# Masked softmax on one core: GpSimd in place of SyncE as the engine that opens and closes the first critical section

## The chip, the cores and the metric

The kernel runs on one core of a Trainium2 chip. The metric is the device time of one launch in microseconds (us). The core has five engines with an instruction stream each: PE (TensorE), DVE (VectorE), ACT (ScalarE), POOL (GpSimd) and SP (SyncE, which computes nothing and here issues transfers). [...] Transfers between the device memory and the on-chip memory are issued from SP, ACT or POOL and are carried out by 16 DMA engines that all of these share.

## The reference

```python
batch, heads, seq_q, seq_k = 16, 8, 256, 256
x       = randn(batch, heads, seq_q, seq_k)           # float32
lengths = randint(seq_k // 2, seq_k, size=batch)      # int32
result  = zeros_like(x)
for b in range(batch):
    n = lengths[b]
    m = x[b, :, :, :n]
    e = exp(m - max(m, axis=-1))
    result[b, :, :, :n] = e / sum(e, axis=-1)
```

Each row of 256 values is a softmax over its first `lengths[b]` values, and zero behind them. The input and the output have 33.55 MB each.

## The kernel before

**Tiling.** One batch is 2048 rows of 256 float32 values, 2 MB. It lies in the on-chip memory as 128 partitions with 16 rows each (`nt = 16`). The tile `xt` has eight slots, each for one batch, so that loads run ahead of the arithmetic and stores behind it. Everything is done in place in `xt`.

**Arithmetic.** For a batch DVE clips the columns from 128 on with a ramp (`down`, line 231, plus the length, line 248), so that what lies behind the length becomes a huge negative number. ACT takes the exponential (lines 374 and 377), for twelve of the sixteen rows of a partition with the row's sum beside it; DVE sums the other four (line 269). DVE then takes the reciprocal (line 279) and multiplies (line 282). In the first batch it clips and waits by halves.

**Transfers.** The lengths come in by one small transfer on ACT's queue (line 142). The first batch comes in as two halves on SP's queue (line 145). The next three come on POOL's queue (line 196), behind a memset (line 191) that waits until DVE has the lengths as a tile (`len_s`, line 239; on the way there lie a cast on DVE, line 236, and a small matmul, line 216). All later loads are issued by POOL in a loop (lines 205 to 211) which reads the length of the batch and branches to one of twelve transfers that differ in the number of columns loaded (line 168). A load waits until the store that last used its slot is done. All 39 stores are issued by SP (line 154), each behind a wait for DVE's multiplication.

**The order around the change.** The order of instructions on each engine is that of the program text, and all waits are written out by hand. For this the kernel's body stands in a critical section (line 106), in which the framework adds no waits of its own. At its two ends, however, the framework adds a few instructions, and they carry line 106 in the profile:

- Opening: one engine, here SP, executes a NOP that increments a semaphore of this engine. Every engine, SP too, then has a branch into the section, and the branch waits for that semaphore (these branches carry line 433).
- Closing: when the opening engine has done its own part of the body, it increments a second semaphore. Every engine has, behind its own part, a drain that waits for this second semaphore and then increments a semaphore of its own; for POOL it is a NOP in place of the drain, because of `no_gpsimd_drain=True`. The opening engine waits for all of these, and executes a closing NOP.

Ahead of the section stands a barrier over all engines (line 422): the four others report to POOL, and POOL then releases them. Behind the section stands a second one, opened and closed by SP, that holds a single wait:

```python
    with tc.tile_critical(no_gpsimd_drain=True):
        nc.sync.wait_ge(s_last, 64)
```

`s_last` counts the stores of the last batch. After it comes the closing barrier of the program (line 433), again with POOL as the engine to which the others report.

The body of the section starts like this on the three engines that issue transfers:

```python
        nc.scalar.dma_start(out=word64, in_=lengths[None, :]).then_inc(s_word, 16)
        for h in range(2):
            s = slice(h * half, (h + 1) * half)
            nc.sync.dma_start(out=xt[:, 0, s], in_=x_f[batch_of(0), :, s]).then_inc(s_ld[h], 16)
...
        nc.gpsimd.iota(
```

SP's part of the body ends with waits for the stores of all batches but the last (lines 157 to 159). POOL's part ends with its last load. ACT and DVE end with a test of the sums that, for this input, leaves a branch untaken (lines 333 and 384).

Of the kernel before, what the change touches and what calls it, by code (L numbers as in the profile page):

```python
# [17 lines left out]
POOL = mybir.EngineType.Pool  # L18
# [3 lines left out]
def kernel(  # L22
# [80 lines left out]
    s_late = sem("s_late")  # L103
    s_last = sem("s_last")
    n_st = [64 * (len(range(par, late, 2)) + 2) for par in range(2)]
    with tc.tile_critical(no_gpsimd_drain=True):  # L106
        s_word = sem("s_word")
        s_ones = sem("s_ones")
        s_lenb = sem("s_lenb")
# [328 lines left out]
```

## Time and profile before

| what | value |
|---|---|
| time, median of 3 runs | 154.49 us (154.41 to 154.68) |
| span of the profiled execution, first to last instruction | 152.8 us |
| the profiled execution's own time | not given; its span lies 1.7 us under the median |
| bytes moved by DMA | 61.57 MB, 403 GB/s over the span |
| DVE, ACT, POOL busy | 134.6, 95.1, 21.3 us |

The profile is that of one execution. An engine's name with a small q behind it (SPq, POOLq) means its sequencer: semaphore instructions, branches, NOPs, drains and the issuing of transfers, which are not counted as busy time. In the view by stretches the DMA share is the time that the packets begun in a stretch took, over that of 16 engines; a full stretch shows about 1.0 and can be a little over it. In the source view a row gives the engine, the instruction, its count, its shortest, median and longest duration in ns, and the starts of the first and the last one in us; a view that is cut to a stretch has only the instructions that run in it.

### The profile page before, as it was taken

The numbers are of one execution on the slowest core, as the hardware profiler recorded it, in microseconds if no ns is written. First come the engines' busy times: TensorE is split into PE (matmuls) and PEld (weight loads), VectorE is DVE, ScalarE is ACT, GpSimd is POOL, SyncE is SP. The second block draws the span as 40 slices with busy tenths as digits, with TensorE's granted clock in tenths as the row PEclk, the third lists the DMA queues.
The fourth block names the chain that finished last, engine by engine and source line by source line (L and its number), as shares of the span: only waits on it lengthen the run. The fifth ranks groups of instructions, "written<-read, shape, count | busy, mean of one in ns | idle before, by whom it ended". The sixth has DMA issues, their size and how long they took to land.

```text
span 152.8 us, 818 instructions
## 1 busy us (share of the span) xinstructions
PE 0.3 (0%) x2; PEld 0.2 (0%) x2; DVE 134.6 (88%) x107; ACT 95.1 (62%) x402; POOL 21.3 (14%) x29
## 2 busy tenths in 40 slices
PE   0000000000000000000000000000000000000000
PEld 0000000000000000000000000000000000000000
DVE  1369999999999999999999999999999999999500
ACT  3096699339394967859393939577593939395000
POOL 4962110030303020030300220302000000000000
DMA  4999999999999999999999999999999999999994
GB/s 107 420 446 433 401 435 347 421 445 420 394 397 422 405 421 411 411 409 405 419 411 418 408 399 419 408 410 423 417 421 419 413 420 422 435 435 442 429 410 187
DMA packets 10646, 61.57 MB, mean 403 GB/s; under 512 B 898, under 2 KB 1010, under 8 KB 7058
## 3 DMA queue, kind: packets, MB, share of 16 engines
q1 hardware_dynamic: 5904, 35.65, 56.7%
q0 software_dynamic: 4736, 25.89, 41.9%
q14 instruction: 4, 0.03, 0.1%
q10 hardware_dynamic: 2, 0.00, 0.0%
HBM read 27.98 MB, written 33.55 MB: 403 GB/s over the span
## 4 chain that ended last, share of the span: by engine, by line
DVE 87%; DMA 5%; issue 1%; SPq 0%; PE 0%
DVE xt L282 48%; DVE xt L248 23%; DVE row_sum L269 12%; DMA xt<-in_x_dram 5%; DVE inv_sum L279 3%; DVE ends L317 0%; SPq L145 0%; DVE bad L320 0%; PE count L218 0%; DVE redo L328 0%; SPq L433 0%; SPq L106 0%
## 5 line engine op out<-in xcount | busy, mean ns | idle before, releaser
L377 ACT ACTIVATE xt<-xt 128x256 f32<-128x256 f32 x192 | 76.6, 400 | 0.2 <-DVE xt L248 0.2
L282 DVE TENSOR_TENSOR xt<-xt,inv_sum 128x2048 f32<-128x2048 f32 x32 | 73.3, 2292 | 1.1
L374 ACT ACTIVATE xt<-xt 128x1024 f32<-128x1024 f32 x16 | 16.9, 1056 | 42.8 <-DVE xt L248 42.8
L248 DVE SCALAR_TENSOR_TENSOR xt<-down,len_s,xt 128x2048 f32<-128x2048 f32 (+1 forms) x17 | 37.7, 2219 | 5.0 <-DMA xt<-in_x_dram 5.0
L377 ACT ACTIVATION_READ_ACCUMULATOR xt<-xt 128x1 f32 x192 | 35.9, 187 | 0.0
L168 POOL DMA_DIRECT2D xt<-in_x_dram x12 | 13.2, 1104 | 84.0 <-DMA xt<-in_x_dram 62.3
L269 DVE TENSOR_REDUCE row_sum<-xt 128x4 f32<-128x1024 f32 x16 | 19.4, 1210 | 0.0
L279 DVE RECIPROCAL inv_sum<-row_sum 128x8 f32<-128x8 f32 x32 | 6.3, 198 | 0.5
L191 POOL MEMSET xt<- 128x1536 f32 x4 | 5.4, 1398 | 1.1 <-DVE len_s L239 1.1
L361 ACT ACT_TABLE_LOAD x1 | 1.3, 1283 | 1.6 <-SPq L106 1.6
L196 POOL DMA_DIRECT2D xt<-in_x_dram x3 | 1.8, 590 | 0.0
L231 DVE TENSOR_SCALAR down<-iota_i 128x256 f32<-128x256 int32 x1 | 0.3, 300 | 1.6 <-POOL iota_i L181 1.6
L317 DVE TENSOR_REDUCE ends<-inv_sum 128x1 f32<-128x256 f32 x2 | 0.7, 408 | 0.0
L236 DVE CAST len_b<-word 1x16 bf16<-1x16 int32 x1 | 0.2, 164 | 0.4 <-DMA word<-in_lengths_dram 0.4
L239 DVE TENSOR_SCALAR len_s<-len_f 128x16 f32<-128x16 f32 x1 | 0.2, 176 | 0.3 <-PE len_f L216 0.3
L218 PE MATMUL count<-bad,ones_c 128*1 128x3 bf16 x1 | 0.2, 165 | 140.8 <-DVE bad L320 140.8
L181 POOL IOTA iota_i<- 128x256 int32 x1 | 0.3, 331 | 0.6 <-SPq L106 0.6
L328 DVE TENSOR_REDUCE redo<-count 1x1 f32<-1x3 f32 x1 | 0.1, 150 | 0.3 <-PE count L218 0.3
L320 DVE TENSOR_SCALAR bad<-ends 128x1 bf16<-128x1 f32 x3 | 0.3, 150 | 0.0
L187 POOL MEMSET seed<- 1x1 f32 x2 | 0.2, 225 | 0.0
L218 PEld LDWEIGHTS count<-bad,ones_c 128*1 128x1 bf16 x1 | 0.1, 79 | 140.8 <-DVE bad L320 140.8
L361 ACT ACTIVATE warm<-const-float32-0.0 128x1 f32<-128x1 f32 x1 | 0.2, 204 | 0.0
(10 smaller groups left out, 1.1 us busy)
## 6 DMA issues: line engine op xcount, KB each, us to landing
out_dram<-xt SPq DMA_DIRECT2D x20, 1024.0 KB
xt<-in_x_dram POOLq DMA_DIRECT2D x4, 2048.0 KB, 16.3
out_dram<-xt SPq DMA_DIRECT2D x15, 512.0 KB
xt<-in_x_dram POOLq DMA_DIRECT2D x3, 1728.0 KB, 16.7
out_dram<-xt SPq DMA_DIRECT2D x2, 2048.0 KB
xt<-in_x_dram POOLq DMA_DIRECT2D x2, 1600.0 KB, 16.0
xt<-in_x_dram POOLq DMA_DIRECT2D x2, 1280.0 KB, 14.7
xt<-in_x_dram SPq DMA_DIRECT2D x2, 1024.0 KB, 6.4
```

Of the source, the lines that this page charges most:

```text
L168: nc.gpsimd.dma_start(out=xt[:, slot, :, :w], in_=x_n[:, b, :, :w]).then_inc(s_sw[par], 16)
L191: nc.gpsimd.memset(xt[:, b, :, low:], 0.0).then_inc(s_fill, 1)
L196: nc.gpsimd.dma_start(out=xt[:, b], in_=x_f[batch_of(b)]).then_inc(s_sw[b - 1] if b < 3 else s_ld[2], 16)
L218: nc.tensor.matmul(count, lhsT=ones_c, rhs=bad, start=True, stop=True).then_inc(s_count, 1)
L248: return nc.vector.scalar_tensor_tensor(out=t, in0=down[:, None, lo:hi].to_broadcast([P, s.stop - s.start, hi - lo]), scalar=len_s[:, batc ...
L269: nc.vector.tensor_reduce(out=row_sum[:, b % slots, :lump], in_=xt[:, b % slots, :lump, :], op=ALU.add, axis=AX,).then_inc(s_exp[0], 1)
L279: step(nc.vector.reciprocal(out=inv_sum[:, b, s], in_=row_sum[:, b % slots, s]))
L282: nc.vector.tensor_tensor(out=t, in0=t, in1=inv_sum[:, b, s, None].to_broadcast([P, half, seq_k]), op=ALU.mult,).then_inc(s_out, 1)
L317: step(nc.vector.tensor_reduce(out=ends[:, k : k + 1], in_=values, op=op, axis=AX))
L361: nc.scalar.activation(out=warm, in_=nc.const_aps.tensor(0.0, (P, 1), F32), func=EXP)
L374: nc.scalar.activation(out=e, in_=e, func=EXP).then_inc(s_lump, 1)
L377: ins = nc.scalar.activation(out=e, in_=e, func=EXP, accum_out=row_sum[:, slot, j : j + 1])
```

## The change

The first section is told to use POOL for its opening and closing; the second section, and everything inside the first, is the same.

```diff
-    with tc.tile_critical(no_gpsimd_drain=True):
+    with tc.tile_critical(sync_engine=POOL, no_gpsimd_drain=True):
         s_word = sem("s_word")
         s_ones = sem("s_ones")
         s_lenb = sem("s_lenb")
```

So the opening NOP, the increment with which the closing starts, and the closing NOP with its waits go from SP's instruction stream to POOL's, and the branches into the section wait for a semaphore of POOL. Each engine keeps its drain (POOL its NOP) at the end of its part.

## Prediction

> **What bounds the kernel now.** I read the page first, then the stretches by time, then the waits of DVE and of SP's queue, and last the chain of waits at the two ends of the run, because the change touches only the ends. The page gives the span, the engines and the bytes.
>
> ```profile
> span 152.8 us, 818 instructions
> PE 0.3 (0%) x2; PEld 0.2 (0%) x2; DVE 134.6 (88%) x107; ACT 95.1 (62%) x402; POOL 21.3 (14%) x29
> DMA packets 10646, 61.57 MB, mean 403 GB/s; under 512 B 898, under 2 KB 1010, under 8 KB 7058
> ```
>
> ```profile
> DVE 87%; DMA 5%; issue 1%; SPq 0%; PE 0%
> ```
>
> ```profile
> 143.74 0.15 DVE redo L328
> ```
>
> DVE is the busiest engine, and the chain of waits puts 87% of the span on it. The last piece of that chain (second fence: start, duration, what) ends at 143.9 us, though, nine microseconds before the span does. The stretches show what fills them (columns: stretch and its length, busy time and count for PE, PEld, DVE, ACT and POOL, clock, DMA share, GB/s).
>
> ```profile
> 2.00:2.10 0.10, 0.00 (x0) 0.00 (x0) 0.00 (x0) 0.10 (x1) 0.00 (x0) 1.00 0.00 0
> 2.10:2.20 0.10, 0.00 (x0) 0.00 (x0) 0.00 (x0) 0.10 (x1) 0.00 (x0) 1.00 1.36 246
> 2.00:4.00 2.00, 0.17 (x1) 0.10 (x1) 0.34 (x2) 1.13 (x2) 0.95 (x1) 1.00 0.93 246
> 4.00:6.00 2.00, 0.00 (x0) 0.00 (x0) 0.00 (x0) 0.00 (x0) 2.00 (x4) 1.00 0.98 410
> 6.00:8.00 2.00, 0.00 (x0) 0.00 (x0) 1.28 (x1) 0.22 (x1) 2.00 (x3) 1.00 1.07 455
> 20.00:24.00 4.00, 0.00 (x0) 0.00 (x0) 3.96 (x4) 4.00 (x16) 0.03 (x1) 1.00 0.92 370
> 30.00:90.00 60.00, 0.00 (x0) 0.00 (x0) 59.28 (x44) 40.91 (x175) 8.09 (x7) 1.00 1.02 413
> 90.00:140.00 50.00, 0.00 (x0) 0.00 (x0) 49.38 (x37) 35.08 (x150) 3.45 (x3) 1.00 1.02 420
> 146.00:150.00 4.00, 0.00 (x0) 0.00 (x0) 0.00 (x0) 0.00 (x0) 0.00 (x0) 1.00 1.00 422
> 150.00:151.00 1.00, 0.00 (x0) 0.00 (x0) 0.00 (x0) 0.00 (x0) 0.00 (x0) 1.00 0.72 303
> ```
>
> The reader is to see the next-to-last number: the 16 DMA engines start moving x between 2.1 and 2.2 us and are then full, at a share of about 1.0, until past 150 us, while all compute engines stand still after 146. So the **bytes** set the end: when they start, and at what rate they go. DVE is nearly as full, and it also begins with those bytes:
>
> ```profile
> DVE xt L248 <- DMA xt<-in_x_dram: 5.0, 2, 3.5
> SPq L433 <- DMA out_dram<-xt: 4.2, 1, 4.2
> ```
>
> DVE's only waits for x are the two halves of the first batch. SP's last wait, 4.2 us, is for the last stores. Whichever of the two one takes as the bound, it hangs on the instant at which SP issues the first x load, and that instant is where the change works. The chain of waits between 0.5 and 1.2 us has it (start, duration, what):
>
> ```profile
> 0.85 0.05 issue
> 0.90 0.01 SPq L106
> 0.92 0.06 issue
> 0.98 0.03 SPq L433
> 1.01 0.12 issue
> 1.14 0.39 SPq L145
> ```
>
> SP is let out of the program's first barrier at about 0.84 (its barrier instruction takes 17 ns by its row below and ends at 0.85), executes the NOP of line 106 at 0.90, passes its own branch into the section at 0.98 and issues the first load at 1.14. The first data follow 0.96 to 1.06 us after that.
>
> **The entry, part by part.** The barrier is opened by GpSimd itself. In the source view of line 422, cut to 0.80 to 0.81 us, the second of GpSimd's barrier instructions is what runs, and cut to 0.80 to 0.85 us it has SP's; the view of line 433 cut to 0.94 to 0.95 us has GpSimd's branch, and cut to 0.93 to 0.95 us ACT's; line 106, over the whole span, has a NOP of each of the two engines.
>
> ```profile
> L422 POOLq EVENT_SEMAPHORE  x1: 17/17/17, 0.8 to 0.8; - x1
> L422 SPq EVENT_SEMAPHORE  x1: 17/17/17, 0.8 to 0.8; - x1
> L433 POOLq COMPARE_BRANCH  x1: 38/38/38, 0.9 to 0.9; - x1
> L433 ACTq COMPARE_BRANCH  x1: 38/38/38, 0.9 to 0.9; - x1
> L106 SPq NOP  x2: 13/13/13, 0.9 to 147.3; - x2
> L106 POOLq NOP  x1: 17/17/17, 147.0 to 147.0; - x1
> ```
>
> So GpSimd frees the others at about 0.80, SP hears of it 0.04 later, and then the opening signal goes back the same way: SP's NOP at 0.90, the branches of ACT and GpSimd at 0.94. The change takes out that second crossing for SP. GpSimd's NOP comes one sequencer step after its barrier instruction; SP's step there is 0.05 (the "issue" row), and I take 0.05 to 0.07, which puts the NOP at 0.86 to 0.88. With 0.04 of crossing the signal is at SP at 0.90 to 0.92. SP, without a NOP of its own, is ready for its branch at 0.85 + 0.05 = 0.90. Its branch then stands at 0.90 to 0.92 in place of 0.98: **0.06 to 0.08 earlier, I take 0.07**. The 4 ns by which GpSimd's NOP is longer is inside that rounding. Both ends: no more than 0.08 can be gained, because SP is not ready before 0.90; and nothing is lost, because GpSimd stood at its branch by 0.94 at the latest, so its NOP cannot be later than that and the signal is at SP by 0.98, as now. The two load issues, the 39 stores behind them on SP's queue and DVE's first mask all move with SP.
>
> The other engines: ACT's branch goes from 0.94 to 0.90 to 0.92, so the load of the lengths, issued on ACT, is about 0.03 earlier. GpSimd now waits for its own signal; SP's own took 0.08 from NOP to branch, so GpSimd's branch is at 0.87 + 0.08 = 0.95, 0.01 later, and up to 0.08 later at the bound above. Behind it on GpSimd are the iota, three kinds of small memset and the first large memset. The lines that wait on them:
>
> ```profile
> POOL xt L191 <- DVE len_s L239: 1.1, 1, 1.1
> DVE down L231 <- POOL iota_i L181: 1.6, 1, 1.6
> DVE len_b L236 <- DMA word<-in_lengths_dram: 0.4, 1, 0.4
> ```
>
> GpSimd waits 1.1 us for the lengths before its first large memset, and DVE, after the mask ramp that needs the iota, waits 0.4 us for the lengths. Those waits hide 0.01 to 0.08; if the cover were gone the price would be those same hundredths. The loads that GpSimd issues behind that memset depend on the lengths, which come 0.03 sooner.
>
> **The exit.** GpSimd now gives the closing signal when its own part is done, after its last load, and its NOP collects the drains of the others; SP keeps its drain. The section can still not be closed before SP has left it, since GpSimd's NOP waits for SP's drain. Rows of the source views of lines 106, 205 and 433, the last cut to 147.3 to 152.2 us:
>
> ```profile
> L205 POOLq COMPARE_BRANCH  x6: 34/48/50, 19.6 to 106.4; - x6
> L106 SPq DRAIN  x1: 7/7/7, 147.1 to 147.1; - x1
> L106 SPq EVENT_SEMAPHORE  x3: 17/28/28, 147.0 to 147.2; - x3
> L433 SPq EVENT_SEMAPHORE  x3: 28/28/4155, 147.4 to 147.6; - x3
> L433 POOLq DRAIN  x1: 478/478/478, 147.1 to 147.1; - x1
> ```
>
> GpSimd leaves its loop at 106.4 and has nothing else to do. All of the closing lies between 147.0 and 147.4, and behind it SP waits from 147.6 for 4.155 us for the last store. One signal may cross once more or once less, 0.04, and several waits move from SP's queue to GpSimd's, where only the drain of 0.478 us stands behind them, ending near 147.6. All of it is inside the 4.155 us, so I cost it at nothing. Without that cover the whole closing is worth 0.4 us. The second section is still opened and closed by SP, so what follows the last store, from 151.7 on, stays as it is.
>
> **Sum.** Entry 0.07 earlier, exit 0. The profiled span of 152.84 us becomes 152.77. The profiled execution's own time is not shown, so I take the 1.65 us between its span and the median of 154.49 as unchanged: 154.49 - 0.07 = **154.42 us**. The runs shown reach from 154.41 to 154.68, so 0.07 is not to be told from no change; about 0.2%, 0.31 us, is what a measurement of this kernel can tell.
>
> **Rivals.** First, no gain: GpSimd reaches its NOP only by 0.94, or the compiler's placement leaves SP's branch where it was; then 154.49. For it speaks that no row shows GpSimd's idle sequencer between 0.82 and 0.94.
>
> Second, slower: the lengths fall behind x. Today ACT's issue goes ahead of SP's:
>
> ```profile
> 1.09 0.52 ACTq L142 DMA_DIRECT2D word<-in_lengths_dram  x1
> 1.14 0.86 SPq L145 DMA_DIRECT2D xt<-in_x_dram  x2
> 4.37 1.76 POOL L196 DMA_DIRECT2D xt<-in_x_dram  x3
> ```
>
> The lead is 0.05 now and about 0.01 afterwards (1.06 against 1.07). If SP gets ahead and the two can't issue at once, the lengths are late by SP's first issue, 0.39 us, and with them GpSimd's memset and its three loads, at 4.37 now. SP's two loads are 2 MB together; the stretches move 0.49 + 0.82 + 0.91 = 2.22 MB by 8 us, so GpSimd's data are already flowing just before 8 us. If they come 0.39 later, the DMA engines run dry for that long: 154.49 + 0.39 = 154.88. [...] Against it: the two issues overlap today, and the lead, though small, stays on ACT's side.
>
> [...]
>
> Third, more gained than the start: the stretch from 20 to 24 us, where the first stores meet the end of the opening loads, runs at share 0.92 and 370 GB/s in place of 1.02 and 413. At 413 it would be 4 x (1 - 370/413) = 0.42 us shorter: 154.42 - 0.42 = 154.00. Against it: loads and stores both move by 0.07, so their relative order has little reason to change.
>
> **How the numbers follow.** Forecast 0.58, no gain 0.12, lengths late 0.14, the stretch mended 0.16. Of the forecast's share, 0.04 is given to runs that scatter past the 0.31 us on the fast side. That makes faster 0.20, within 0.2% 0.66, slower 0.14. The range reaches to both outer cases, 154.0 to 154.9; the likeliest one's own is 154.41 to 154.49 by the bounds 0.08 and 0, and with the scatter of the runs shown 154.3 to 154.65.
>
> **What would show it.** Right: GpSimd's NOP near 0.87, SP's branch near 0.91 and its first load near 1.07, first data 0.07 earlier, DMA share about 1.0 up to 150 us, SP's last wait still above 4 us. The lengths' rival shows as DVE's wait for them growing from 0.4 towards 0.8 and a gap in the DMA share near 8 us. The third shows as a share of 1.0 between 20 and 24 us. The forecast is wrong if SP's first load does not move, if the last wait of SP shrinks towards nothing, or if the rate in the long stretches shifts by more than the 0.2% that would drown the 0.07.

## The result, and the profile after

The changed kernel is **slower** by a little: 154.79 us against 154.63 us (medians of 13 runs each, in turn on one chip), a ratio of 1.0017 with a 95% interval of 1.0009 to 1.0025. Over all runs whose span is on record, on several chips, the median is 154.77 us (36 runs) against 154.53 us (128 runs of the kernel before).

The entry did what the prediction worked out. The chain of waits of the changed kernel between 0.5 and 1.2 us (start, duration, what):

```profile
0.74 0.06 issue
0.80 0.02 POOLq L422
0.82 0.06 issue
0.88 0.03 POOLq L106
0.91 0.02 issue
0.92 0.03 SPq L433
0.95 0.12 issue
1.08 0.39 SPq L145
```

GpSimd's NOP stands at 0.88, SP's branch at 0.92 where it was at 0.98, and the first x load at 1.08 where it was at 1.14. The stretches of the changed kernel show that the data follow: between 2.10 and 2.20 us there is more than twice the traffic of before (573 against 246 GB/s), and the long stretches run at the same rates.

```profile
2.10:2.20 0.10, 0.00 (x0) 0.00 (x0) 0.00 (x0) 0.10 (x1) 0.00 (x0) 1.00 3.34 573
20.00:24.00 4.00, 0.00 (x0) 0.00 (x0) 3.97 (x3) 3.97 (x18) 0.54 (x1) 1.00 0.96 380
30.00:90.00 60.00, 0.00 (x0) 0.00 (x0) 59.27 (x44) 40.91 (x175) 8.08 (x7) 1.00 1.02 413
146.00:150.00 4.00, 0.00 (x0) 0.00 (x0) 0.00 (x0) 0.00 (x0) 0.00 (x0) 1.00 1.00 424
```

The closing is with GpSimd now. Line 106 of the changed kernel:

```profile
L106 POOLq NOP  x3: 13/17/17, 0.9 to 147.2; - x3
L106 POOLq EVENT_SEMAPHORE  x3: 17/43/43, 107.1 to 147.1; - x3
L106 PEldq DRAIN  x1: 218/218/218, 143.0 to 143.0; - x1
L106 ACTq DRAIN  x1: 8/8/8, 144.3 to 144.3; - x1
L106 DVEq DRAIN  x1: 17/17/17, 144.5 to 144.5; - x1
L106 SPq DRAIN  x1: 7/7/7, 147.0 to 147.0; - x1
```

GpSimd gives the closing signal at 107.1 us, the drains follow at 143.0 to 147.0 where in the kernel before they all stand at 147.0 to 147.1, and the closing NOP stands at 147.2 where SP's stood at 147.3.

The end differs in two ways. First, the source view of line 433, SP alone, from 151.9 us on: the kernel before,

```profile
L433 SPq DRAIN  x3: 7/7/7, 152.1 to 152.4; - x3
L433 SPq EVENT_SEMAPHORE  x2: 17/17/17, 152.3 to 152.8; - x2
```

and the changed kernel:

```profile
L433 SPq EVENT_SEMAPHORE  x3: 17/17/28, 152.1 to 152.9; - x3
L433 SPq DRAIN  x3: 7/7/7, 152.2 to 152.5; - x3
```

SP has one semaphore instruction more behind the last store. It names semaphores that SP has waited for already at 147.3 us, and it starts 0.04 us behind the end of the instruction ahead of it. The same instruction is in the trace of a kernel below in which ACT opens and closes the first section, and in none in which SP does. So it comes with the collecting of the drains on another engine; why the framework adds it is not shown.

Second, the time that isn't in the span at all. Each run has its time and its span; time minus span is what a launch takes outside the instructions that the profile lists:

| | runs | median time | median span | time minus span, mean (standard deviation) |
|---|---|---|---|---|
| kernel before | 128 | 154.53 | 152.8 | 1.68 (0.06) |
| changed kernel | 36 | 154.77 | 152.9 | 1.87 (0.03) |

The spans are nearly level (means 0.07 us apart), which fits 0.06 us gained at the entry and about 0.07 lost behind the last store. The gain is not to be seen at the end of this pair of executions: SP's branch behind the last store stands at 151.7 us in both. The loss of 0.19 us lies **outside** the instructions that the profile shows. One row of the trace hints at it: the transfer view of the kernel before, cut to 154.4 to 154.5 us, 1.6 us behind its last profiled instruction, has one transfer of the kind that the profile names `instruction`, called a fetch from here on (82 GB/s over the 0.1 us, so 8 KB),

```profile
q14 instruction: 1, 0.01, 33.2%
```

and the changed kernel, cut to 151.4 to 156 us, has no transfer at all behind its end.

```profile
DMA packets 0, 0.00 MB, mean 0 GB/s; under 512 B 0, under 2 KB 0, under 8 KB 0
```

### The profile page after: what moved, and what is told of

It reads as the page before. It is cut to its first block, busy times and chain, and to the rows that moved or that the text cites. A ratio compares the mean times of both kernels' runs of the same rounds, so it can differ in the third digit from the quotient of the medians.

```text
span 152.9 us, 819 instructions
## 1 busy us (share of the span) xinstructions
PE 0.3 (0%) x2; PEld 0.2 (0%) x2; DVE 134.7 (88%) x107; ACT 95.0 (62%) x402; POOL 21.3 (14%) x29
## 4 chain that ended last, share of the span: by engine, by line
DVE 87%; DMA 5%; issue 1%; SPq 0%; PE 0%; POOLq 0%
DVE xt L282 48%; DVE xt L248 23%; DVE row_sum L269 12%; DMA xt<-in_x_dram 5%; DVE inv_sum L279 3%; DVE ends L317 0%; SPq L145 0%; DVE bad L320 0%; PE count L218 0%; DVE redo L328 0%; SPq L433 0%; POOLq L106 0%; POOLq L422 0%
```

## Experiments

All comparisons are with runs of the kernel before on the same chip, in turn. "Length" is the number of SP's instructions in the compiled program: 79 before, 75 in the changed kernel, because the opening NOP, the closing increment and the collecting of the drains went to GpSimd and one wait came in at the end. The traces list two fewer each, 77 and 73. Added instructions are increments of semaphores that nobody waits for; they are called hidden where SP would wait anyway.

### First four: control, repeat, and two ends

The control is the kernel before, unedited.

> The kernel before, once more, as a control. Every theory: the ratio to the kernel before is 1.000 with its interval around it. The profile adds a second sample of what the trace of before showed: first x load on SP at 1.14 us, first data between 2.1 and 2.2 us, DVE's last piece near 143.7, SP's wait for the last store over at 151.7 us, span 152.8 us. What differs between this profile and the first is what one execution scatters by.

Ratio 0.9992 (0.9979 to 1.0005), median 154.56 us against 154.56; its profiled execution has a span of 153.1, so 0.3 us is what one execution scatters by.

The changed kernel, unedited.

> The changed kernel once more, on the chip of the other three. Tail theory (the one further semaphore instruction of SP behind the last store, 0.06 us, is all that the change costs, and the earlier entry isn't carried to the end): ratio 1.0004, SP's wait for the last store over at 151.7 us. Early-load theory (loading x 0.06 us earlier brings DVE's chain and the stores forward, and the mixed traffic then runs slower): ratio 1.001 to 1.002, last store at 151.7 us or later although the data start 0.07 us earlier.

Ratio 1.0019 (1.0001 to 1.0036), median 154.72 against 154.56, time minus span 1.88. The loss repeats.

```diff
+        nc.sync.sem_inc(s_pad[0], 1)
         for h in range(2):
             s = slice(h * half, (h + 1) * half)
```

> The changed kernel with one semaphore instruction of SP, about 0.06 us, ahead of its two x loads, so that these are issued at 1.14 us as in the kernel before; the longer tail stays. Tail theory: no faster than the changed kernel, 1.0004 against the kernel before. Early-load theory: the 0.1 to 0.2 us come back and 0.06 us of tail are left, 1.0004 as well, but 0.001 less than the changed kernel run beside it.

The first load went to 1.18 us; ratio 1.0015 (0.9993 to 1.0038), median 154.80, time minus span 1.85. Nothing came back, and the time outside the span, where no load runs, is as long as in the changed kernel. So nothing speaks for the theory that early loads slow the traffic; the interval is too wide to exclude the 0.001 that it asked for.

```diff
         nc.sync.wait_ge(s_last, 64)
+        for k in range(4):
+            nc.sync.sem_inc(s_pad[k], 1)
```

> The kernel before with four more semaphore instructions of SP behind its wait for the last store, and nothing else. Tail theory: each costs one step of the sequencer, 0.06 to 0.07 us, whole: the span is 0.24 to 0.28 us longer, ratio 1.0016 to 1.0018. If what stands behind the last store is hidden by something (the other engines' part of the closing barrier): ratio 1.000.

Ratio 1.0036 (1.0025 to 1.0048): 0.55 us, twice the expectation. The source views of lines 408 and 436 (the closing barrier in this file), SP alone, say why:

```profile
L408 SPq EVENT_SEMAPHORE  x4: 17/17/17, 151.7 to 151.9; - x4
L436 SPq EVENT_SEMAPHORE  x5: 17/17/28, 152.0 to 153.5; - x5
L436 SPq DRAIN  x3: 7/7/130, 152.6 to 153.2; - x3
```

The steps take 0.07 us each (three from 151.7 to 151.9; the first increment rides on the wait for the last store). Three waits that in the kernel before stand ahead of that wait came behind it here (five semaphore instructions of line 436 in place of the two shown above), so there are six steps more and not four, about 0.4 us. And one drain, 130 ns in place of 7, came late. That stall was expected by no theory. Time minus span was 1.63, the smallest so far. Both together led to the next question: does the length of a stream decide?

### Second four: whose length

```diff
                 pick(v_len, bass.ds(b, 1), bass.ds(n % slots, 1), par, widths + [seq_k], landed)
+        for k in range(4):
+            nc.gpsimd.sem_inc(s_pad[k], 1)
```

> The kernel before with four more semaphore instructions of GpSimd behind its last load, where it is idle from 106 us on; with the branch that they bring its stream is five instructions longer, as in the changed kernel. The runs so far put the loss of 0.16 us outside the profiled span: time minus span is on average 1.67 to 1.73 us for the kernel before and 1.87 to 1.88 for the changed one. Theory that the length of GpSimd's stream makes it: time minus span 1.87, ratio 1.001. Theory that the length of SP's stream makes it: 1.70, ratio 1.000.

Ratio 0.9998 (0.9984 to 1.0012), time minus span 1.67. GpSimd's length does not bring the loss.

```diff
+        for k in range(4):
+            nc.sync.sem_inc(s_pad[k], 1)
         for par in range(2):
             nc.sync.wait_ge(s_st[par], n_st[par])
```

> The changed kernel with four more semaphore instructions of SP ahead of its waits for the stores (line 157), where it waits for 3.9 us; its stream is then as long as in the kernel before. Length of SP's stream: time minus span falls from 1.87 to 1.70 and the time to that of the kernel before. Length of GpSimd's stream, or neither: time minus span stays at 1.87, ratio 1.001.

Ratio 0.9999 (0.9985 to 1.0012), 154.52 against 154.51 us, time minus span 1.71. **Four idle instructions on SP remove the whole loss**; the changed opening and closing are still there.

```diff
-    with tc.tile_critical(no_gpsimd_drain=True):
+    with tc.tile_critical(sync_engine=ACT, no_gpsimd_drain=True):
```

> ACT opens and closes the first section in place of SP. SP's stream is as short as in the changed kernel, GpSimd's as in the kernel before, ACT's five instructions longer. Length of SP's stream: time minus span 1.87. Length of GpSimd's: 1.70. Tail theory: the span has the same further semaphore instruction behind the last store as the changed kernel, 0.06 us.

Ratio 1.0031 (1.0005 to 1.0056), median 154.82, time minus span 1.87. The same loss outside, with GpSimd's stream as long as before. (The ratio is pulled up by four long runs of twelve; the profiled one is one of them, with a span of 154.3.)

The four hidden instructions of the last but one kernel, in the kernel before:

> The kernel before with four more semaphore instructions of SP ahead of line 157, hidden there. The run with four instructions behind the last store had a time minus span of 1.63 and, in its profile, a stall of SP of about 0.3 us inside the closing barrier. Length of SP's stream: the same again, time minus span 1.63, and the stall in the closing barrier, with nothing added behind the last store; ratio 1.001 to 1.002. Otherwise: ratio 1.000 and no stall.

Ratio 1.0026 (1.0011 to 1.0040), time minus span 1.62, and the stall is there. Line 436 on SP, cut to 152.3 to 152.8 us, and the kernel before at the same place (line 433, cut to 152.3 to 152.5):

```profile
L436 SPq EVENT_SEMAPHORE  x1: 17/17/17, 152.3 to 152.3; - x1
L436 SPq DRAIN  x1: 130/130/130, 152.7 to 152.7; - x1
```

```profile
L433 SPq EVENT_SEMAPHORE  x1: 17/17/17, 152.3 to 152.3; - x1
L433 SPq DRAIN  x1: 7/7/7, 152.4 to 152.4; - x1
```

The drain behind the same semaphore instruction starts 0.3 us later, and takes 130 ns. Nothing but the number of SP's instructions ahead of it was changed.

### Third four: does the stall move as counted?

Hidden instructions ahead of line 157 again, now 17 in the kernel before and 21 and 12 in the changed one:

> The kernel before with 17 semaphore instructions of SP hidden ahead of line 157, which makes its stream 96 instructions long in place of 79. Theory of the boundary: at one fixed place of SP's instruction stream SP stalls for about 0.3 us; with 83 instructions it lay in front of SP's last drain of the closing barrier, so each instruction added ahead moves it one instruction earlier, and with 96 it lies before the wait for the last store, where SP waits 4 us anyway. Then time minus span is 1.62, the span has no stall, and the time is 0.05 to 0.1 us below the kernel before, ratio 0.9995. Rival (the effect comes and goes with the length in some other way): time minus span 1.7 or more, or a stall in the closing barrier.

> The changed kernel with 21 hidden semaphore instructions of SP, 96 as well. Boundary theory: time minus span 1.62 in place of 1.87, no stall in the span, ratio 0.9995 to 1.000 against the kernel before and 0.15 to 0.25 us below the changed kernel. Compared with the other run of 96 instructions it shows the change without the boundary: entry 0.06 us earlier and tail 0.06 us longer, together nothing; 0.06 us slower if the entry isn't carried to the end. Rival: 1.70 or 1.87 outside.

> The changed kernel with 12 hidden semaphore instructions of SP, 87 in all. Boundary theory: the boundary lies between the wait for the last store and the closing barrier, so the profile shows a gap of about 0.3 us on SP there, four instructions earlier than with 83, time minus span 1.62, ratio 1.001 to 1.002: slower than with 79 and than with 96. Rival (longer is better): between the times of 79 and 96.

The place was right in all three traces. With 87 (12 hidden in the changed kernel), lines 409 and 436 on SP, the second cut to 152.7 to 153.2 us:

```profile
L409 SPq NOP  x1: 17/17/17, 152.6 to 152.6; - x1
L436 SPq EVENT_SEMAPHORE  x1: 28/28/28, 153.0 to 153.0; - x1
L436 SPq DRAIN  x2: 7/22/37, 153.1 to 153.2; - x2
```

A gap of 0.4 us in front of the sixth instruction from the end, as counted. With 96 in the kernel before, line 107 on SP from 146 to 148.5 us has its three semaphore instructions, which span 147.0 to 147.2 in the kernel before, stretched over 0.6 us:

```profile
L107 SPq EVENT_SEMAPHORE  x3: 17/28/28, 146.9 to 147.6; - x3
```

Time minus span was 1.62 in all three, as expected. The times were not: 154.99 us and 1.0035 (1.0022 to 1.0049) for the first, 155.07 and 1.0035 (1.0023 to 1.0047) for the second, where 0.9995 to 1.000 was expected; 154.99 and 1.0029 (1.0019 to 1.0040) for the third, where 1.001 to 1.002 was. With 96 the stall is hidden behind SP's 4 us wait and outside nothing is lost, but the span is 0.6 us longer (means 153.40 and 153.43 against 152.78).

The fourth tested whether the start of the loads reaches the end. Its four instructions stand ahead of the x loads, 13 more ahead of line 157:

> The kernel before with four semaphore instructions of SP ahead of its first x load and 13 hidden ones, 96 in all: the first x load is issued 0.27 to 0.4 us later. If the start of the loads is carried whole to the end: the span is 0.27 to 0.4 us longer than in the other run of the kernel before with 96. If the end does not follow the start: the span is the same.

The loads on SP's timeline, the kernel before with 96 first:

```profile
1.14 0.86 SPq L146 DMA_DIRECT2D xt<-in_x_dram  x2
```

```profile
1.42 0.86 SPq L148 DMA_DIRECT2D xt<-in_x_dram  x2
```

0.28 us later; the mean span is 153.72 against 153.40 with the same length (five runs each), 0.32 longer. The start is **carried whole** to the end.

### Fourth four: the stall far from the end

Hidden instructions behind the two x loads, where SP is idle for 12 us, 40 in the kernel before and 44 in the changed one:

```diff
             nc.sync.dma_start(out=xt[:, 0, s], in_=x_f[batch_of(0), :, s]).then_inc(s_ld[h], 16)
+        for k in range(40):
+            nc.sync.sem_inc(s_pad[k % 8], 1)
```

> The kernel before with 40 semaphore instructions of SP behind its two x loads, where it is idle from 2 to 14 us; its stream has 119 instructions. Boundary theory: the stall and the instruction fetch that follows it lie among SP's stores in the middle of the run, where SP waits for DVE and one 8 KB fetch is nothing. Then time minus span 1.62, no gap on SP behind the last store, no fetch behind 120 us, and the time 0.05 to 0.1 us below the kernel before, ratio 0.9993 to 0.9997. If the stall is not tied to a place in the stream: 1.000 or more.

> The changed kernel with 44 such instructions at the same place, 119 as well. Boundary theory: time minus span 1.62, and the change's loss is gone: the same as the other run with 119 to within 0.06 us, 0.2 to 0.3 us below the changed kernel. If the loss lies in what the change itself does (the opening, the closing, the order of the first loads): still 0.15 us above the other run with 119.

And 27 ahead of line 157 in the kernel before, 106 in all:

> The kernel before with 27 hidden instructions ahead of line 157, 106 in all, where 17 made it slower by 0.5 us although the stall was hidden. Theory of the late fetch (there the 8 KB fetch ran at 150.9 us, among the last stores, and one of the 16 DMA engines reported the last store about 0.45 us after the others): the stall moves among the hidden instructions near 144 us, the fetch to about 147 us, the straggler goes, and the time is 0.05 to 0.1 us below the kernel before. Rival (the hidden instructions themselves, or a long stream, delay the end): slower by 0.5 us as with 17.

The changed kernel stood beside them once more:

> The changed kernel again, on the chip of these three, for the comparison. All theories: ratio 1.001 to 1.002, time minus span 1.87, no instruction fetch behind 120 us in the trace.

The last came out as expected: 1.0019 (1.0000 to 1.0038), 1.86 outside. The other three had their stall where it was counted, at 94.2, 85.6 and 144.3 us, and their fetch 3.4 us or less behind its end: the kernel before with 119 has a fetch at 97.8 us and none behind 120. Outside, they lost nothing (1.61, 1.64, 1.61). In time all three missed: 155.20 us and 1.0041 (1.0027 to 1.0055), 155.11 and 1.0035 (1.0023 to 1.0046), 154.92 and 1.0016 (0.9995 to 1.0036). With equal lengths the changed kernel does not show the loss of 0.16 to 0.27 us: it is 0.09 us below the kernel before with 119 (155.11 against 155.20) and 0.08 above with 96 (155.07 against 154.99). With five to seven runs each, 0.1 us is not resolved; that the time outside is level (1.64 against 1.61, 1.62 in both with 96) says more.

What else is new in them can be seen in the transfer views from 10 to 152 us, the kernel before and then the one with 119, and in the stretches of the latter at its end:

```profile
q14 instruction: 4, 0.03, 0.1%
```

```profile
q14 instruction: 5, 0.04, 0.1%
```

```profile
151.00:151.20 0.20, 0.00 (x0) 0.00 (x0) 0.00 (x0) 0.00 (x0) 0.00 (x0) 1.00 0.00 0
151.20:151.40 0.20, 0.00 (x0) 0.00 (x0) 0.00 (x0) 0.00 (x0) 0.00 (x0) 1.00 0.11 41
151.40:151.60 0.20, 0.00 (x0) 0.00 (x0) 0.00 (x0) 0.00 (x0) 0.00 (x0) 1.00 0.00 0
151.60:151.80 0.20, 0.00 (x0) 0.00 (x0) 0.00 (x0) 0.00 (x0) 0.00 (x0) 1.00 0.10 41
```

41 GB/s over 0.2 us is one packet of 8 KB. Single packets still start behind 151.2 and 151.6, after nearly all the traffic is over; the kernel before starts none of this size after 151.0:

```profile
151.00:151.20 0.20, 0.00 (x0) 0.00 (x0) 0.00 (x0) 0.00 (x0) 0.00 (x0) 1.00 0.01 0
151.20:151.40 0.20, 0.00 (x0) 0.00 (x0) 0.00 (x0) 0.00 (x0) 0.00 (x0) 1.00 0.01 0
```

All six kernels with a fifth fetch ahead of the end of the last store have median spans 0.4 to 0.7 us longer than the kernel before beside them (for the one with late x loads, without their 0.3). It is not shown that the fetch does it. Late single packets do not go with it: the kernel before with 96 has the fetch and none of them (first line), and the changed kernel with 87 has them (the other two) although its fetch comes only at 153.6 us, behind the last store.

```profile
151.20:151.40 0.20, 0.00 (x0) 0.00 (x0) 0.00 (x0) 0.00 (x0) 0.00 (x0) 1.00 0.01 0
```

```profile
151.20:151.40 0.20, 0.00 (x0) 0.00 (x0) 0.00 (x0) 0.00 (x0) 0.00 (x0) 1.00 0.10 41
151.40:151.60 0.20, 0.00 (x0) 0.00 (x0) 0.00 (x0) 0.00 (x0) 0.00 (x0) 1.00 0.10 41
```

The median span with 87 is 0.6 us longer as well, of which the stall is about 0.4. A rival, that many added instructions lengthen the run by themselves, was not separated from the fetch. What lengthens these spans stays open.

### Last two: between 75 and 83

Seven and six hidden instructions ahead of line 157 in the changed kernel:

> The changed kernel with 7 hidden semaphore instructions of SP ahead of line 157, 82 in all. By the count (83: the stall in front of the next to last instruction of SP's closing barrier, 87: in front of the sixth from the end, 96: the fifteenth) the stall now lies in front of the very last one, where SP waits 0.37 us for GpSimd's release anyway, and the fetch behind it comes after the last store. Boundary theory: time minus span 1.62, the span at most 0.1 us longer, time 154.5 to 154.6, as the kernel before or 0.05 us below it and 0.2 us below the changed kernel. Rival (each instruction short of 83 is as good as 79): time minus span 1.70.

> The same with 6, 81 in all: the stall lies just behind the last profiled instruction. Boundary theory: no gap on SP in the span, time minus span between 1.62 and 1.87; if SP's first instructions behind the span wait for nothing, the stall shows whole, about 1.9; if they wait for other engines as with 79, about 1.65 to 1.7 and the time is that of the kernel before.

With 82: 154.49 us against 154.58, ratio 1.0004 (0.9990 to 1.0017), time minus span 1.62. With 81: 154.68, 1.0022 (1.0004 to 1.0039), time minus span 1.61, below what was expected. Its profiled span is 152.8, but the median of its spans is 153.05; what lengthens them isn't known. So 82 takes the loss outside the span away, and is not shown to be faster than the kernel before. No version tried beats both.

All lengths together:

| SP's length | kernels | stall on SP | time minus span, mean |
|---|---|---|---|
| 75 | changed (three sets of runs); ACT opens | not in the span | 1.86 to 1.88; 1.87 |
| 76 | changed, x late | not in the span | 1.85 |
| 79 | before; control; GpSimd +4; changed, SP +4 | not in the span | 1.68; 1.73; 1.67; 1.71 |
| 81, 82 | changed, SP +6 and +7 | 81: not in the span; 82: in SP's last wait, 0.42 us where it is 0.36 otherwise | 1.61, 1.62 |
| 83 | before, tail +4 and SP +4 | second instruction from the end | 1.63, 1.62 |
| 87 | changed, SP +12 | sixth from the end | 1.62 |
| 96, 106, 119 | before and changed | before the wait for the last store; with 119, among the stores | 1.61 to 1.64 |

From 83 on, the stall is in the trace, and moves one instruction earlier with each one added: in all nine traces with 83 to 119 it stands in front of the 80th of SP's listed instructions, 0.40 to 0.42 us long. With 81 and less it would lie behind the last profiled instruction, in the part that the profile doesn't list. With 81 the time outside is still 1.61; with 79 to 75 it grows, to 0.25 us over the 1.62 that is left when the stall lies elsewhere. One sign supports that it is the same stall. The fetch, too, falls the later behind the end of the span the shorter the stream is: 0.3 us behind it with 83, 0.6 with 82, 1.0 with 81, 1.6 to 1.8 in four traces with 79, 1.9 with 76. With 75, the changed kernel's own length, the four traces list none. So for the changed kernel itself the stall is an extrapolation of the count; so is the reason why 79 hides most of it. What the runs show is that the loss comes and goes with the number of SP's instructions.

In the transfer views the fetches have a queue of their own (q14, 0.03 MB in four packets between 10 and 152 us in the kernel before). That SP's stall and the fetch behind it belong together is my inference from the order of the two and from the stall's fixed place; no run shows what the stall comes from. What is measured is that SP stood for 0.40 to 0.42 us, and that with 83 (SP +4) and 87 instructions, where nothing hid it, the median spans are 0.45 and 0.6 us longer than those of the kernel before beside them.

## Why the prediction was wrong

**What bounds the kernel** was right as far as it was tested: the loads' start is carried whole to the end (0.28 us later gave 0.32).

**The entry** was right in each step up to SP's load: NOP at 0.88 (0.86 to 0.88 predicted), SP's branch at 0.92 (0.90 to 0.92), first load at 1.08 (1.07). It is worth 0.06 us. Off by a little were the other two: ACT's issue came 0.01 us earlier and not 0.03, and GpSimd's iota 0.04 later (1.28 against 1.24) and not 0.01; the waits behind them covered both.

**The lengths' rival** had its condition fulfilled and no price. On the timeline of the changed kernel ACT's issue no longer has a lead:

```profile
1.08 0.39 SPq L145 DMA_DIRECT2D xt<-in_x_dram  x1
1.08 0.52 ACTq L142 DMA_DIRECT2D word<-in_lengths_dram  x1
```

Yet neither issue takes longer than before, and DVE's wait for the lengths stayed at 0.4 us:

```profile
DVE len_b L236 <- DMA word<-in_lengths_dram: 0.4, 1, 0.4
SPq L433 <- DMA out_dram<-xt: 4.3, 1, 4.3
```

So the 0.39 us that I would have charged for two issues at once isn't there: both start at 1.08, SP's takes 0.39 us and ACT's 0.52, as they did with starts 0.05 apart. The 154.88 took it that the two can't issue at once; that was my assumption, and no run shows it. The second line is SP's last wait, still above 4 us, so the exit's cover was as forecast. Of the third rival little came: the stretch from 20 to 24 us runs at 380 GB/s in place of 370, and no 0.42 us came off the span.

**"So what follows the last store, from 151.7 on, stays as it is"**: this failed first. I counted the closing instructions that the change names and gave the whole closing to the cover of SP's wait; but with the collecting of the drains on GpSimd (and likewise on ACT) SP has one wait more where there is no cover. It costs one step of the sequencer, 0.07 us, and eats the gain.

**"I take the 1.65 us between its span and the median as unchanged"**: this failed second, and it is the loss. Outside the span 1.68 became 1.87, 0.19 us more, because SP's stream became four instructions shorter. Four hidden instructions on SP brought it back to 1.71 and the time to that of the kernel before; four more on GpSimd changed nothing. Corrected, the sum is -0.06 + 0.07 + 0.19 = +0.20 us; the three ratios of the changed kernel, 1.0017, 1.0019 and 1.0019, are 0.26 to 0.29 us and the differences of the medians 0.16, 0.16 and 0.27.

None of the three rivals was this one. That 154.79 us lies inside the range of 154.0 to 154.9 is luck: its upper end stood there for the late lengths, which did not happen, and the kernel before itself read 154.63 us in this comparison, not 154.49. The profile of before held a hint: a stretch outside the span as long as 1.65 us, with nothing in it that I could name, is a term with unknown bounds and not a constant.

## What to carry to other kernels

When a change moves instructions from one sequencer to another, count the stream of each engine and look at time minus span as a term of its own: here it went from 1.68 to 1.87 us with nothing to see among the profiled instructions. In this kernel nothing covers what SP does behind the last store, so one more wait there was paid in full, 0.07 us. A kernel that differs by 0.2% may owe it to the length of an engine's stream and not to the idea that was tried; a few idle instructions on the same engine help to tell the two apart, but 17 and more of them lengthened the span here, by 0.4 to 0.7 us.

## What was not expected of the hardware

- SP stalls for 0.4 us at one fixed place of its instruction stream, in front of its 80th listed instruction, in nine traces of programs with 83 to 119 instructions on SP; an 8 KB fetch follows 0.6 to 3.4 us later.
- The time outside the profiled span is 1.61 us with 81 instructions on SP and 1.87 with 75, in kernels that otherwise do the same.
- One fetch more during the run went with a span longer by 0.4 to 0.7 us; why is open.
- Two transfers issued at the same time to the hundredth, from SP and from ACT, did not delay each other by anything that the rows show: from 1.08 us on they took 0.39 and 0.52 us, and the same with starts at 1.14 and 1.09.
